# Wide and narrow matmuls of the queries, keys and MLP up halves in another order, and a last weight quarter stored 64 bytes later

## The chip, the cores and the metric

The kernel runs on one core of a Trainium2 chip. The metric is the device time of one execution in microseconds (us); lower is better. Before the change it is 740.41 us, the median of three runs between 740.17 and 740.46.

## The reference

An encoder trunk of two layers over 256 positions of 1024 features. Layer 0 mixes with two kinds of attention, layer 1 with a dilated attention of three head groups, and each is followed by an MLP:

```
for layer in range(2):
    xn = rms_norm(x, norm_mix[layer])
    x  = x + (even_mixer(xn, ...) if layer == 0 else odd_mixer(xn, ...))
    x  = x + square(relu(rms_norm(x, norm_mlp[layer]) @ w1[layer])) @ w2[layer]
return rms_norm(x, norm_final)

odd_mixer: hcat = xn @ w_in            # 3 groups x (queries, keys, values) x 16 heads x 64
           q, k = rope(q), rope(k)     # of every group
           out  = dilated_attention(q, k, v) @ w_o
```

The change touches two of these products: `xn @ w1` of both MLPs, and the queries and keys of `odd_mixer`.

## The kernel before, in words

**Split products.** Every matmul operand is a float32 value cut into a high part and a low remainder, and a product is taken as hi x hi + hi x lo + lo x hi. In the two places here that is done as a *wide* matmul, 512 moving columns, whose stationary operand is the high part of a weight tile and whose moving operand holds hi and lo of the activations side by side, and a *narrow* one, 256 columns, whose stationary operand is the low part of the weights. Both add up in one PSUM bank of 512 columns. With 1024 features in 8 tiles of 128 (`KT`), one tile of 128 output features needs 8 wide and 8 narrow matmuls.

**The weights' way.** A piece is 128 x 2048 floats. SyncE loads it (`load_weight`, L181), then ScalarE casts the high part into a tile `whi` (L215) and VectorE subtracts for the low part `wlo` (L216), each in four quarters of 512 columns (`split_piece`). Three `whi` and three `wlo` tiles exist; each is 128 columns larger than a piece, and `SHIFTS` says by how many floats a piece is moved inside its tile: `LINE`, 16 floats or 64 bytes, for the low part of `w1` and `w_oqk` (the queries' and keys' weights), nothing for their high part.

**The MLP's up half.** `up(j)`, 16 units in each MLP, makes 256 hidden features from one piece of `w1`: for j > 0 all 16 wide matmuls (L405), 8 for each of two banks, then all 16 narrow ones (L408). Unit 0 goes over the input features in three stretches, because these come late there.

**Queries and keys.** `qk_steps` makes one piece, two tiles of features (f = 0, 1), in four steps. For each f a step of 6 wide matmuls (L926), then one of 2 wide and 8 narrow (L929); f = 0 is then emptied from its PSUM bank by a copy on ScalarE (`side`, L934) and an addition on VectorE (L935), f = 1 by one reduction on VectorE (L937). Then `rope` turns the piece into queries or keys (L945 to L961). There are 8 units of heads with three pieces each, 24 pieces in all; `weave` puts the scores (L996), the transposes of the probabilities (L1016) and the mix with the values (L1027, L1032) of the unit before between the steps.

**What sets the order.** Each engine runs its instructions in one fixed order, made when the program is built, mostly that in which they are written; a `high_priority` block lets its instructions go ahead of others of their engine. Waits between engines are semaphores.

Of the kernel before, what the change touches and what calls it, by code (L numbers as in the profile page):

```python
# [17 lines left out]
F32R = mybir.dt.float32r  # L18
AF = mybir.ActivationFunctionType
ALU = mybir.AluOpType  # L20
# [3 lines left out]
P = 128  # L24
D = 1024
KT = D // P
T = 256
# [7 lines left out]
WCH = 2048  # L35
# [4 lines left out]
WPARTS = 4  # L40
NORM_PRIO = 300
# [2 lines left out]


LINE = 16
SHIFTS = {"w1": (0, LINE), "w_oqk": (0, LINE), "w_qk": (LINE, LINE), "w_oe": (LINE, LINE), "w_oo": (LINE, LINE)}

QK_ORDER = (0, 2, 1)
# [25 lines left out]
def trunk(ctx, tc, a, out):  # L75
    nc = tc.nc
# [8 lines left out]
    wsp = ctx.enter_context(tc.tile_pool(name="wsp", bufs=WBUFS))  # L85
    ps = ctx.enter_context(tc.tile_pool(name="ps", bufs=4, space=PSUM))

    def scratch(shape, name):

        n = int(np.prod(shape))  # L90
        v = work.tile([P, 512], F32, tag="scratch", name=name, bufs=12)[:, :n]
        if len(shape) == 2:
            v = v.rearrange("p (a b) -> p a b", b=shape[1])
        return v
# [13 lines left out]
    def bank(tag):  # L108
        return ps.tile([P, 512], F32, tag=tag, name=tag)
# [32 lines left out]
    specs = []  # L142

    def plan(name, n):
        for j in range(a[name].shape[0]):
            specs.append((a[name][j], n, SHIFTS.get(name, (0, 0))))

    def plan_mlp(layer):
        for j in (0, 1):
            specs.append((a["w1"][layer, j], WCH, SHIFTS["w1"]))  # L150
        for j in range(2, 16):
            specs.append((a["w1"][layer, j], WCH, SHIFTS["w1"]))
            specs.append((a["w2"][layer, j - 2], WCH, (0, 0)))
        for j in (14, 15):
            specs.append((a["w2"][layer, j], WCH, (0, 0)))

    CV = 416 + 512
    plan("w_cv", 2 * CV)
# [5 lines left out]
    plan("w_oe", 2 * D)  # L164
    plan_mlp(0)
    for kind, *at in odd_weights():
        specs.append((a[kind][tuple(at)], WCH, SHIFTS.get(kind, (0, 0))))
    plan("w_oo", 2 * D)
    plan_mlp(1)

    parts = {}
    state = {"loaded": 0, "split": 0, "used": 0}

    def load_weight(edges=None, earlier=lambda i: None):
        j = state["loaded"]
        src, n, _ = specs[j]
        raw = wraw.tile([P, WCH], F32, tag="raw", name="raw")
        edges = edges or (0, n)
        for i, c in enumerate(slice(*e) for e in zip(edges, edges[1:])):
            earlier(i)  # L180
            nc.sync.dma_start(raw[:, c], src[:, c])  # L181
        parts[j] = [raw, None, None]
        state["loaded"] = j + 1

    def split_tiles(j):
        return [wsp.tile([P, WCH + P], F32R, tag=n, name=n)[:, o:o + WCH] for n, o in zip(("whi", "wlo"), specs[j][2])]

    def cut(j, i, n):
        w = specs[j][1] // n
        return slice(i * w, (i + 1) * w)  # L190

    def split_piece(eng=None):
        j, i = divmod(state["split"], WPARTS)
        if i == 0:
            parts[j][1:] = split_tiles(j)
        raw, hi, lo = (z[:, cut(j, i, WPARTS)] for z in parts[j])
        state["split"] += 1
        return split(hi, lo, raw, eng)

# [49 lines left out]
    def two(z):  # L249
        return z.rearrange("p (f n) -> p f n", f=2)  # L250
# [137 lines left out]
    def mlp(mp, xT, s, invert, tail, make_down, beside=lambda j: None):  # L388


        hs = {}

        def up(j):
            w = weight()

            pu = [bank("w") for _ in range(2)]

            ranges = [range(4), range(4, 6), range(6, 8)] if j == 0 else [range(8)]  # L400
            cut_of = lambda k, f: slice(k * 256 + f * P, k * 256 + f * P + P)
            for ks in ranges:
                for f in range(2):
                    for k in ks:
                        nc.tensor.matmul(two(pu[f]), w[0][:, cut_of(k, f)], xT[2][:, k], start=k == 0, stop=False)  # L405
            for f in range(2):
                for k in range(KT):
                    nc.tensor.matmul(pu[f][:, 0:T], w[1][:, cut_of(k, f)], xT[0][:, k, :], start=False, stop=k == KT - 1)  # L408
            side, u = scratch([2, T], "side"), scratch([2, T], "u")
            for f in range(2):  # L410
                nc.scalar.copy(side[:, f], pu[f][:, T:2 * T])  # L411
                nc.vector.tensor_tensor(u[:, f], pu[f][:, 0:T], side[:, f], op=ALU.add)  # L412
            u, h = u.rearrange("p f n -> p (f n)"), scratch([512], "hsq")
            nc.vector.scalar_tensor_tensor(h, u, 0.0, u, ALU.max, ALU.mult)  # L414
            hs[j] = tuple(mp.tile([P, 512], F32R, tag=n, name=n, bufs=4) for n in ("hh", "hl"))
            split(*hs[j], h)

        squares = square_steps(s)
        for j in range(3):
            up(j)  # L420
            run_all(squares[2 * j - 2:2 * j])
        inv = invert()
        accs = open_accs()
        down = make_down(accs, hs)
        for j in range(tail[0]):
            w = weight()
            for f in range(2):
                down(j, w, f)
            if j + 3 < 16:
                up(j + 3)  # L430
            beside(j)
        return accs, hs, inv, {j: weight() for j in tail}
# [414 lines left out]
    def odd(op, xT, s):  # L847
        xh, xl, xp = xT
# [8 lines left out]
        for i in range(2):  # L857
            z = op.tile([P, 2, 4, P], F32, name=f"k12_{i}")
# [53 lines left out]
        def qk_steps(d, js=QK_ORDER):  # L912


            hold = {}

            def gemm(b, f, half):
                if f == 0 and half == 0:
                    hold["w"], hold["q"] = weight(), op.tile([P, 2, T], F32, tag="qk32", name="qk32", bufs=2)
                if half == 0:  # L920
                    hold["p"] = bank("acc")
                (wh, wl), pq, q32 = hold["w"], hold["p"], hold["q"]

                cut_of = lambda k: slice((f * KT + k) * P, (f * KT + k + 1) * P)
                for k in (range(0, 6), range(6, KT))[half]:
                    nc.tensor.matmul(two(pq), wh[:, cut_of(k)], xp[:, k], start=k == 0, stop=False)  # L926
                if half == 1:
                    for k in range(KT):
                        nc.tensor.matmul(pq[:, 0:T], wl[:, cut_of(k)], xh[:, k, :], start=False, stop=k == KT - 1)  # L929
                if half == 1:  # L930
                    with tc.high_priority(NORM_PRIO):
                        if f == 0:
                            side = scratch([T], "side")
                            nc.scalar.copy(side, pq[:, T:2 * T])  # L934
                            nc.vector.tensor_tensor(q32[:, f], pq[:, 0:T], side, op=ALU.add)  # L935
                        else:
                            nc.vector.tensor_reduce(q32[:, f], pq.rearrange("p (h n) -> p n h", h=2), axis=mybir.AxisListType.X, op=ALU.add)  # L937
                if f == 1 and half == 1:

                    with tc.high_priority(NORM_PRIO if b == QK_ORDER[-1] else 0):  # L940
                        rope(b, q32.rearrange("p f n -> p (f n)"))

            def rope(b, pq):

                sw, r1 = op.tile([P, 512], F32, tag="swap", name="sw", bufs=2), scratch([2, T], "r1")  # L945
                change = nc.scalar.copy if b == 1 else nc.sync.dma_start
                for r in range(0, P, 64):
                    change(sw[r:r + 32], pq[r + 32:r + 64])
                    change(sw[r + 32:r + 64], pq[r:r + 32])
                sw = sw.rearrange("p (f n) -> p f n", f=2)  # L950
                nc.vector.tensor_tensor(r1, pq.rearrange("p (f n) -> p f n", f=2), cosT.unsqueeze(1).broadcast_to([P, 2, T]), op=ALU.mult)
                nc.vector.tensor_tensor(sw, sw, sinT.unsqueeze(1).broadcast_to([P, 2, T]), op=ALU.mult)
                if b == 0:
                    nc.vector.tensor_tensor(r1, r1, sw, op=ALU.add)
                    split(d["q0h"], d["q0l"], r1)
                elif b == 1:
                    nc.vector.tensor_tensor(d["q12"], r1, sw, op=ALU.add)
                else:
                    for r in (0, 64):
                        cut = lambda z: z[r:r + 64].rearrange("p j (c n) -> p j c n", n=64)  # L960
                        nc.vector.tensor_tensor(d["k12"][r:r + 64, :, :, r:r + 64], cut(r1), cut(sw), op=ALU.add)  # L961

            return [lambda v=(b, f, h): gemm(*v) for b in js for f in range(2) for h in range(2)]

        def made_beside(plan, units):

# [97 lines left out]
        for u in range(7):  # L1064
            side = attend(u, units[u])
# [17 lines left out]
    xT, s = hand_over(accs, last, 1)  # L1083
# [103 lines left out]
```

## Time and profile before

| | |
|---|---|
| median of three runs | 740.41 us |
| the profiled execution | 740.37 us |
| its span, first to last instruction | 738.6 us |
| mean granted TensorE clock | 0.997 |
| PE (TensorE) busy | 730.7 us, 99% |
| PEld (TensorE weight loads) busy | 630.6 us, 85% |
| DVE (VectorE) busy | 540.8 us, 73% |
| ACT (ScalarE) busy | 471.3 us, 64% |

The 1.77 us between span and execution lie before the first and after the last instruction. Matmuls overlap on PE, so the length of one (390 ns for a wide one) is not its price; its price is the distance from its start to the start of the next. The chain of waits, which the profile follows back from the last instruction, gives it for runs of equal matmuls: a line `1.84 PE acc L926 x8` says that eight wide matmuls took 1.84 us from the start of the first to the start of what came next.

### The profile page before, as it was taken

The numbers are of one execution on the slowest core, as the hardware profiler recorded it, in microseconds if no ns is written. First come the engines' busy times: TensorE is split into PE (matmuls) and PEld (weight loads), VectorE is DVE, ScalarE is ACT, GpSimd is POOL, SyncE is SP. The second block draws the span as 40 slices with busy tenths as digits, with TensorE's granted clock in tenths as the row PEclk, the third lists the DMA queues.
The fourth block names the chain that finished last, engine by engine and source line by source line (L and its number), as shares of the span: only waits on it lengthen the run. The fifth ranks groups of instructions, "written<-read, shape, count | busy, mean of one in ns | idle before, by whom it ended". The sixth has DMA issues, their size and how long they took to land.

```text
span 738.6 us, 11982 instructions
## 1 busy us (share of the span) xinstructions
PE 730.7 (99%) x4539; PEld 630.6 (85%) x4539; DVE 540.8 (73%) x1100; ACT 471.3 (64%) x1020; POOL 8.3 (1%) x20
## 2 busy tenths in 40 slices
PE   9999999999999999999999999999999999999996
PEld 6998998888888887888888888888898888888885
DVE  6788859766665666789968886989559765665674
ACT  6788967554455456468877668687857455455441
POOL 0100000000000001000000000000000000000000
PEclk9999999999999999999999999999999999999998
DMA  8773335565555554645664544455546555555501
GB/s 288 319 256 116 115 114 172 178 222 171 193 206 177 199 195 154 232 156 178 205 226 147 207 160 179 143 192 175 181 159 221 180 174 197 193 177 189 210 1 57
DMA packets 24585, 133.17 MB, mean 180 GB/s; under 512 B 3664, under 2 KB 4816, under 8 KB 10192
## 3 DMA queue, kind: packets, MB, share of 16 engines
q1 hardware_dynamic: 24384, 132.28, 51.5%
q8 instruction: 35, 0.57, 0.3%
q14 instruction: 22, 0.18, 0.1%
q10 hardware_dynamic: 144, 0.13, 0.1%
HBM read 127.16 MB, written 1.05 MB: 174 GB/s over the span
## 4 chain that ended last, share of the span: by engine, by line
PE 96%; issue 1%; ACT 1%; DMA 1%; SPq 0%; DVE 0%; POOLq 0%; POOL 0%
PE w L405 16%; PE acc L219 13%; PE acc L220 13%; PE acc L221 13%; PE acc L926 12%; PE w L408 8%; PE acc L929 6%; PE acc L572 2%; PE w L228 1%; PE w L1016 1%; PE w L219 1%; PE w L783 1%; PE w L220 1%; PE w L221 1%; PE w L996 1%
## 5 line engine op out<-in xcount | busy, mean ns | idle before, releaser
L216 DVE TENSOR_TENSOR wlo<-raw,whi 128x512 fp32r<-128x512 f32 (+2 forms) x471 | 303.9, 682 | 68.8 <-ACT whi L215 68.0
L215 ACT CAST whi<-raw 128x512 fp32r<-128x512 f32 (+2 forms) x471 | 261.8, 614 | 138.2 <-PE acc L221 57.4
L405 PE MATMUL w<-pair,whi 128*128 128x512 f32 x512 | 122.0, 390 | 0.0
L405 PEld LDWEIGHTS w<-pair,whi 128*128 128x128 f32 x512 | 95.4, 188 | 20.1 <-DVE pair L256 0.6
L926 PE MATMUL acc<-pair,whi 128*128 128x512 f32 x384 | 100.9, 399 | 0.0
L219 PE MATMUL acc<-whi,hh 128*128 128x512 f32 x250 | 98.1, 392 | 0.0
L220 PE MATMUL acc<-wlo,hh 128*128 128x512 f32 x250 | 97.8, 391 | 0.0
L221 PE MATMUL acc<-whi,hl 128*128 128x512 f32 x250 | 97.6, 390 | 0.0
L926 PEld LDWEIGHTS acc<-pair,whi 128*128 128x128 f32 x384 | 67.7, 188 | 12.0 <-issue 0.2
L408 PEld LDWEIGHTS w<-pair,wlo 128*128 128x128 f32 x512 | 64.8, 189 | 2.5
L412 DVE TENSOR_TENSOR u<-w,side 128x256 f32<-128x256 f32 x64 | 27.0, 422 | 54.1 <-ACT side L411 53.8
L408 PE MATMUL w<-pair,wlo 128*128 128x256 f32 x512 | 65.5, 281 | 0.0
L215 ACT CAST hh<-hsq 128x512 fp32r<-128x512 f32 x32 | 19.9, 622 | 57.9 <-DVE hsq L414 57.9
L221 PEld LDWEIGHTS acc<-whi,hl 128*128 128x128 f32 x250 | 47.0, 188 | 9.8
L929 PEld LDWEIGHTS acc<-pair,wlo 128*128 128x128 f32 x384 | 51.8, 188 | 4.0
L219 PEld LDWEIGHTS acc<-whi,hh 128*128 128x128 f32 x250 | 47.1, 188 | 8.9
L220 PEld LDWEIGHTS acc<-wlo,hh 128*128 128x128 f32 x250 | 47.1, 188 | 8.6
L929 PE MATMUL acc<-pair,wlo 128*128 128x256 f32 x384 | 52.6, 280 | 0.0
L219 PE MATMUL acc<-whi,pair 128*128 128x512 f32 x80 | 32.3, 404 | 0.0
L220 PE MATMUL acc<-wlo,pair 128*128 128x512 f32 x80 | 31.3, 391 | 0.0
L221 PE MATMUL acc<-whi,pair 128*128 128x512 f32 x80 | 31.2, 390 | 0.0
L1005 DVE CUSTOM_DVE_ANT_0 sn<-w,mask 128x384 f32<-128x384 f32 x32 | 17.6, 551 | 10.9 <-PE w L996 10.9
(220 smaller groups left out, 1104.4 us busy)
## 6 DMA issues: line engine op xcount, KB each, us to landing
raw<-in_w SPq DMA_DIRECT2D x64, 1024.0 KB, 4.9
raw<-in_w_oqk SPq DMA_DIRECT2D x24, 1024.0 KB, 5.0
raw<-in_w_ov SPq DMA_DIRECT2D x12, 1024.0 KB, 5.0
raw<-in_w_qk SPq DMA_DIRECT2D x4, 1024.0 KB, 9.0
raw<-in_w_oe SPq DMA_DIRECT2D x4, 1024.0 KB, 5.0
sw<-qk SPq DMA_DIRECT2D x64, 64.0 KB, 2.0
raw<-in_w_oo SPq DMA_DIRECT2D x4, 1024.0 KB, 5.3
bias<-in_rpb SPq DMA_DIRECT2D x8, 256.0 KB, 3.7
```

The costliest lines, as they stand in the source:

```text
L215: a = nc.scalar.copy(hi, src).ins
L216: return a, (eng or nc.vector).tensor_tensor(lo, src, hi.bitcast(F32), op=ALU.subtract).ins
L219: nc.tensor.matmul(o, sh, mh, start=first, stop=False)
L220: nc.tensor.matmul(o, sh, ml, start=False, stop=False)
L221: nc.tensor.matmul(o, sl, mh, start=False, stop=last)
L405: nc.tensor.matmul(two(pu[f]), w[0][:, cut_of(k, f)], xT[2][:, k], start=k == 0, stop=False)
L408: nc.tensor.matmul(pu[f][:, 0:T], w[1][:, cut_of(k, f)], xT[0][:, k, :], start=False, stop=k == KT - 1)
L412: nc.vector.tensor_tensor(u[:, f], pu[f][:, 0:T], side[:, f], op=ALU.add)
L572: nc.tensor.matmul(o[:, 0:n], xs[i], (w[1], w[1], w[2])[i], start=(k, i) == (0, 0), stop=(k, i) == (KT - 1, 2))
L926: nc.tensor.matmul(two(pq), wh[:, cut_of(k)], xp[:, k], start=k == 0, stop=False)
L929: nc.tensor.matmul(pq[:, 0:T], wl[:, cut_of(k)], xh[:, k, :], start=False, stop=k == KT - 1)
L1005: nc.vector.tensor_tensor_reduce(out=sn, in0=ss[j][:, 0:384], in1=mask[:, i, :], op0=ALU.add, op1=ALU.min, scale=-(HD ** -0.5), scalar=3e3 ...
```

## The change

Three things, and no instruction is added or taken out.

1. **Order of a piece of queries and keys.** The four steps become: 6 wide of f = 0; 2 wide of f = 0 and 4 wide of f = 1; 4 wide of f = 1 and 4 narrow of f = 0; 4 narrow of f = 0, 8 narrow of f = 1, with the emptying of both banks and the rope. So 16 wide matmuls stand ahead of 16 narrow ones, on two PSUM banks, unless something is woven in.
2. **Order of the MLP's up half**, for j > 0: both f over the input features 0 to 5, then both over 6 and 7 (before: 0 to 7 of one f, then of the other). Still 16 wide, then 16 narrow.
3. **The last quarter of `whi`** of `w1` and `w_oqk` is stored 64 bytes later than the other three, and is read there. It is what the last four wide matmuls ahead of a narrow run load: input features 6 and 7 of both f in the MLP (unit 0 too), features 4 to 7 of f = 1 in the queries and keys.

```diff
@@ plan_mlp, and the same for the pieces of odd_weights() @@
-            specs.append((a["w1"][layer, j], WCH, SHIFTS["w1"]))
+            specs.append((a["w1"][layer, j], WCH, SHIFTS["w1"], True))
-        specs.append((a[kind][tuple(at)], WCH, SHIFTS.get(kind, (0, 0))))
+        specs.append((a[kind][tuple(at)], WCH, SHIFTS.get(kind, (0, 0)), kind == "w_oqk"))
@@ split_tiles, split_piece @@
+    def late(c):
+        return slice(c.start + LINE, c.stop + LINE)
...
+        if specs[j][3] and i == WPARTS - 1:
+            hi = parts[j][1][:, late(cut(j, i, WPARTS))]
@@ up @@
-            ranges = [range(4), range(4, 6), range(6, 8)] if j == 0 else [range(8)]
+            ranges = [range(4), range(4, 6), range(6, 8)] if j == 0 else [range(6), range(6, 8)]
...
-                        nc.tensor.matmul(two(pu[f]), w[0][:, cut_of(k, f)], xT[2][:, k], start=k == 0, stop=False)
+                        nc.tensor.matmul(two(pu[f]), w[0][:, late(cut_of(k, f)) if k >= 6 else cut_of(k, f)], xT[2][:, k], start=k == 0, stop=False)
@@ qk_steps @@
+            def wide(f, ks):
+                for k in ks:
+                    c = slice((f * KT + k) * P, (f * KT + k + 1) * P)
+                    nc.tensor.matmul(two(hold["p"][f]), hold["w"][0][:, late(c) if f == 1 and k >= 4 else c], xp[:, k], start=k == 0, stop=False)
...
+                if step == 0:
...
+                    hold["p"] = [bank("acc"), None]
+                    wide(0, range(0, 6))
+                elif step == 1:
+                    wide(0, range(6, KT))
+                    hold["p"][1] = bank("acc")
+                    wide(1, range(0, 4))
+                elif step == 2:
+                    wide(1, range(4, KT))
+                    narrow(0, range(0, 4))
+                else:
+                    narrow(0, range(4, KT))
+                    empty(0)
+                    narrow(1, range(KT))
+                    empty(1)
...
```

In the changed file the wide matmuls of the queries and keys are line L930, the narrow ones L935, the copy `side` L942; scores are L1022 instead of L996, transposes L1042 instead of L1016, the mix L1053 and L1058 instead of L1027 and L1032, the casts L225 instead of L215, the MLP's wide and narrow matmuls L415 and L418 instead of L405 and L408.

On TensorE, in the first unit of attention, right after the scores of unit 0 (`acc<-pair,whi` are wide matmuls, `acc<-pair,wlo` narrow ones, `w<-ident,pp` transposes). Before:

```order
L996 MATMUL w<-k_0_3258,q_3264 64x128 x8
L926 MATMUL acc<-pair,whi 128x512 x2
L929 MATMUL acc<-pair,wlo 128x256 x8
L926 MATMUL acc<-pair,whi 128x512 x8
L929 MATMUL acc<-pair,wlo 128x256 x8
L926 MATMUL acc<-pair,whi 128x512 x6
L1016 MATMUL w<-ident,pp 128x128 x3
L926 MATMUL acc<-pair,whi 128x512 x2
L929 MATMUL acc<-pair,wlo 128x256 x8
L1016 MATMUL w<-ident,pp 128x128 x3
L926 MATMUL acc<-pair,whi 128x512 x8
L929 MATMUL acc<-pair,wlo 128x256 x8
```
After:

```order
L1022 MATMUL w<-k_0_3258,q_3264 64x128 x8
L930 MATMUL acc<-pair,whi 128x512 x10
L935 MATMUL acc<-pair,wlo 128x256 x16
L930 MATMUL acc<-pair,whi 128x512 x6
L1042 MATMUL w<-ident,pp 128x128 x3
L930 MATMUL acc<-pair,whi 128x512 x6
L1042 MATMUL w<-ident,pp 128x128 x3
L930 MATMUL acc<-pair,whi 128x512 x4
L935 MATMUL acc<-pair,wlo 128x256 x16
```
The narrow matmuls stand in runs of 16 instead of 8, and the transposes between wide matmuls.

On TensorE again, one unit later, after scores and mix (`acc<-pts,v`). Before:

```order
L996 MATMUL w<-k_1_3260,q_3637 64x128 x8
L1027 MATMUL acc<-pts,v_3435 64x128 x4
L1032 MATMUL acc<-pts,v_3438 64x64 x4
L1027 MATMUL acc<-pts,v_3435 64x128 x4
L1032 MATMUL acc<-pts,v_3438 64x64 x4
L926 MATMUL acc<-pair,whi 128x512 x8
L929 MATMUL acc<-pair,wlo 128x256 x8
L926 MATMUL acc<-pair,whi 128x512 x8
L929 MATMUL acc<-pair,wlo 128x256 x8
L1016 MATMUL w<-ident,pp 128x128 x3
```
After:

```order
L1022 MATMUL w<-k_1_3260,q_3637 64x128 x8
L1053 MATMUL acc<-pts,v_3435 64x128 x4
L1058 MATMUL acc<-pts,v_3438 64x64 x4
L1053 MATMUL acc<-pts,v_3435 64x128 x4
L1058 MATMUL acc<-pts,v_3438 64x64 x4
L930 MATMUL acc<-pair,whi 128x512 x16
L935 MATMUL acc<-pair,wlo 128x256 x16
L1042 MATMUL w<-ident,pp 128x128 x3
L930 MATMUL acc<-pair,whi 128x512 x12
L1042 MATMUL w<-ident,pp 128x128 x3
```
Two runs of 8 wide and 8 narrow have become one of 16 and 16, and the transposes no longer follow a narrow run only.

On ScalarE in the middle of the queries and keys (`side<-acc` is the copy that empties f = 0, `whi<-raw` are casts of weight quarters, `pts<-w` copies of transposed probabilities). Before:

```order
L215 CAST whi<-raw 128x512 x4
L1018 COPY pts<-w 128x384
L934 COPY side<-acc 128x256
L1018 COPY pts<-w 128x384
L215 CAST whi<-raw 128x512 x4
L215 CAST q0h<-r_5149 128x512
L1018 COPY pts<-w 128x384
L934 COPY side<-acc 128x256
```
After:

```order
L225 CAST whi<-raw 128x512
L942 COPY side<-acc 128x256
L225 CAST whi<-raw 128x512 x3
L1044 COPY pts<-w 128x384 x2
L225 CAST whi<-raw 128x512 x2
L942 COPY side<-acc 128x256
L225 CAST whi<-raw 128x512 x2
```
The copy stands between casts of the next piece; it now comes near the end of its own.

## Rows read from the trace of the kernel before

**Rows 1.** The page: busy time by engine; the last chain's shares by engine, line.

```profile
PE 730.7 (99%) x4539; PEld 630.6 (85%) x4539; DVE 540.8 (73%) x1100; ACT 471.3 (64%) x1020; POOL 8.3 (1%) x20
...
PE 96%; issue 1%; ACT 1%; DMA 1%; SPq 0%; DVE 0%; POOLq 0%; POOL 0%
PE w L405 16%; PE acc L219 13%; PE acc L220 13%; PE acc L221 13%; PE acc L926 12%; PE w L408 8%; PE acc L929 6%; PE acc L572 2%; PE w L228 1%; PE w L1016 1%; PE w L219 1%; PE w L783 1%; PE w L220 1%; PE w L221 1%; PE w L996 1%
```

**Rows 2.** Costliest groups on the page: matmuls, count, busy us, mean ns.

```profile
L405 PE MATMUL w<-pair,whi 128*128 128x512 f32 x512 | 122.0, 390 | 0.0
...
L926 PE MATMUL acc<-pair,whi 128*128 128x512 f32 x384 | 100.9, 399 | 0.0
```

**Rows 3.** PE's load waits: line, releaser, total us, times, longest us.

```profile
PEld w L405 <- DVE pair L256: 0.6, 2, 0.4
...
PEld acc L926 <- issue: 0.2, 1, 0.2
```

**Rows 4.** The chain in time (start us, us, what): queries, keys, transposes.

```profile
320.79 1.84 PE acc L926 x8
322.62 0.94 PE acc L929 x8
...
348.58 1.86 PE acc L926 x8
```

**Rows 5.** The same chain after the scores and the mix of a unit.

```profile
360.63 0.23 PE acc L1032 x8
360.86 2.05 PE acc L926 x8
362.91 0.91 PE acc L929 x8
```

**Rows 6.** The chain in the second MLP: a settled unit of the up half.

```profile
588.20 3.62 PE w L405 x16
591.83 1.89 PE w L408 x16
```

**Rows 7.** The chain in the second MLP: its first units of up.

```profile
553.76 2.06 PE w L405 x9
...
555.82 2.15 PE w L405 x8
557.98 1.83 PE w L408 x16
```

**Rows 8.** PE's timeline (start us, us, what), last stage, operands not shifted.

```profile
728.12 0.28 PE L220 MATMUL w<-wlo,hh 128*128 128x256 f32 x1
...
732.20 0.28 PE L221 MATMUL w<-whi,hl 128*128 128x256 f32 x1
```

**Rows 9.** PE's timeline, first layer, narrow matmuls with shifted loads.

```profile
26.41 0.28 PE L220 MATMUL w<-pair,whi 128*128 128x256 f32 x1
...
30.41 0.28 PE L221 MATMUL w<-pair,wlo 128*128 128x256 f32 x1
...
31.10 0.28 PE L220 MATMUL w<-pair,whi 128*128 128x256 f32 x1
...
34.95 0.28 PE L221 MATMUL acc<-pair,wlo 128*128 128x256 f32 x1
...
35.32 0.36 PE L219 MATMUL acc<-pair,whi 128*128 128x256 f32 x1
35.52 0.28 PE L220 MATMUL acc<-pair,whi 128*128 128x256 f32 x1
```

**Rows 10.** The timeline of all engines where a unit's scores follow its last query.

```profile
475.83 0.68 DVE L957 TENSOR_TENSOR q<-r,sw 128x512 f32<-128x512 f32 x1
...
477.25 1.09 PE L996 MATMUL w<-k,q 128*64 128x128 f32 x16
```

**Rows 11.** Costliest groups on the page: the operations that split the weights.

```profile
L216 DVE TENSOR_TENSOR wlo<-raw,whi 128x512 fp32r<-128x512 f32 (+2 forms) x471 | 303.9, 682 | 68.8 <-ACT whi L215 68.0
L215 ACT CAST whi<-raw 128x512 fp32r<-128x512 f32 (+2 forms) x471 | 261.8, 614 | 138.2 <-PE acc L221 57.4
```

More of the change, by code (lines that the diff above doesn't have):

```diff
@@ L145, in plan @@
         for j in range(a[name].shape[0]):
-            specs.append((a[name][j], n, SHIFTS.get(name, (0, 0))))
+            specs.append((a[name][j], n, SHIFTS.get(name, (0, 0)), False))
     def plan_mlp(layer):
         for j in (0, 1):
-            specs.append((a["w1"][layer, j], WCH, SHIFTS["w1"]))
+            specs.append((a["w1"][layer, j], WCH, SHIFTS["w1"], True))
         for j in range(2, 16):
-            specs.append((a["w1"][layer, j], WCH, SHIFTS["w1"]))
-            specs.append((a["w2"][layer, j - 2], WCH, (0, 0)))
+            specs.append((a["w1"][layer, j], WCH, SHIFTS["w1"], True))
+            specs.append((a["w2"][layer, j - 2], WCH, (0, 0), False))
         for j in (14, 15):
-            specs.append((a["w2"][layer, j], WCH, (0, 0)))
+            specs.append((a["w2"][layer, j], WCH, (0, 0), False))
     CV = 416 + 512
@@ L175, in load_weight @@
         j = state["loaded"]
-        src, n, _ = specs[j]
+        src, n = specs[j][:2]
         raw = wraw.tile([P, WCH], F32, tag="raw", name="raw")
@@ L185, in split_tiles @@
     def split_tiles(j):
-        return [wsp.tile([P, WCH + P], F32R, tag=n, name=n)[:, o:o + WCH] for n, o in zip(("whi", "wlo"), specs[j][2])]
+        z = [wsp.tile([P, WCH + P], F32R, tag=n, name=n) for n in ("whi", "wlo")]
+        return [z[0][:, specs[j][2][0]:specs[j][2][0] + WCH + (LINE if specs[j][3] else 0)], z[1][:, specs[j][2][1]:specs[j][2][1] + WCH]]
+    def late(c):
+        return slice(c.start + LINE, c.stop + LINE)
     def cut(j, i, n):
@@ L915, in qk_steps @@
             hold = {}
-            def gemm(b, f, half):
-                if f == 0 and half == 0:
-                    hold["w"], hold["q"] = weight(), op.tile([P, 2, T], F32, tag="qk32", name="qk32", bufs=2)
[L920 to L938, printed above, removed]
@@ new lines, in wide, with narrow @@
+            def wide(f, ks):
+                for k in ks:
+                    c = slice((f * KT + k) * P, (f * KT + k + 1) * P)
+                    nc.tensor.matmul(two(hold["p"][f]), hold["w"][0][:, late(c) if f == 1 and k >= 4 else c], xp[:, k], start=k == 0, stop=False)
+            def narrow(f, ks):
+                for k in ks:
+                    c = slice((f * KT + k) * P, (f * KT + k + 1) * P)
+                    nc.tensor.matmul(hold["p"][f][:, 0:T], hold["w"][1][:, c], xh[:, k, :], start=False, stop=k == KT - 1)
@@ new lines, in empty @@
+            def empty(f):
+                pq, q32 = hold["p"][f], hold["q"]
+                with tc.high_priority(NORM_PRIO):
+                    if f == 0:
+                        side = scratch([T], "side")
+                        nc.scalar.copy(side, pq[:, T:2 * T])
+                        nc.vector.tensor_tensor(q32[:, f], pq[:, 0:T], side, op=ALU.add)
+                    else:
+                        nc.vector.tensor_reduce(q32[:, f], pq.rearrange("p (h n) -> p n h", h=2), axis=mybir.AxisListType.X, op=ALU.add)
@@ new lines, in gemm @@
+            def gemm(b, step):
+                if step == 0:
+                    hold["w"], hold["q"] = weight(), op.tile([P, 2, T], F32, tag="qk32", name="qk32", bufs=2)
+                    hold["p"] = [bank("acc"), None]
[7 more added lines that the diff above has]
+                    narrow(0, range(0, 4))
+                else:
+                    narrow(0, range(4, KT))
+                    empty(0)
+                    narrow(1, range(KT))
+                    empty(1)
@@ L940, in gemm @@
                     with tc.high_priority(NORM_PRIO if b == QK_ORDER[-1] else 0):
-                        rope(b, q32.rearrange("p f n -> p (f n)"))
+                        rope(b, hold["q"].rearrange("p f n -> p (f n)"))
             def rope(b, pq):
@@ L961, in rope @@
                         nc.vector.tensor_tensor(d["k12"][r:r + 64, :, :, r:r + 64], cut(r1), cut(sw), op=ALU.add)
-            return [lambda v=(b, f, h): gemm(*v) for b in js for f in range(2) for h in range(2)]
+            return [lambda v=(b, i): gemm(*v) for b in js for i in range(4)]
         def made_beside(plan, units):
```

## The prediction

> **What bounds the kernel now.** I read the page first. PE is busy for 99% of the span, and the chain that ended last runs on PE for 96% of it [rows 1]. In the page's costliest groups the wide matmuls of the two places that the change touches stand among the first, 512 of L405 and 384 of L926, with no idle time ahead of them [rows 2]; as many narrow ones, L408 and L929, belong to them. Their shares of the chain are 16 + 8 + 12 + 6 = 42% [rows 1], 310 us. Then I asked for the waits of the weight loads: the largest that touches these lines is 0.6 us in two waits, for activations, and for the queries and keys 0.2 us of "issue" [rows 3]. So no other engine holds PE up there, and the change can only be worth what it does to the pace of PE itself. For that I read the chain in order of time, which gives how long a run of equal matmuls took from its first start to the next start.
>
> **Paces that the trace shows.** A settled wide matmul: 16 in 3.62 us, 0.2263 each [rows 6]. Eight wide after eight narrow take 1.84 us where 8 x 0.2263 is 1.81, so starting again after narrow ones costs 0.03; after transposes 1.86, 0.05 [rows 4]; after a unit's scores and mix 2.05, 0.24 [rows 5]. A narrow matmul has more than one pace, and it holds for a whole run. After settled wide ones 16 take 1.89 us [rows 6] and 8 take 0.94 [rows 4]; after wide ones that were disturbed just before, 8 take 0.91 [rows 5], and in the second MLP 16 take 1.83 behind 17 wide that needed 2.06 + 2.15 us instead of 3.85 [rows 7]. The timeline of the first layer, where the loads are moved by the same 64 bytes, shows both paces ahead of and behind a short break: 34 starts from 26.41 to 30.41 us, 0.1176 each, and 34 from 31.10 to 34.95, 0.1132 each. In the last stage, where no operand is moved, it is 34 starts from 728.12 to 732.20, 0.1200 each [rows 8, 9]. So the same shape of matmul runs at 0.1200, 0.1176 or 0.1132 us without any wait, and what differs is where its loads lie and what ran just ahead. I read that as a phase between loads and matmuls, which a disturbance of a few ns can move.
>
> **The change part by part.** The sum is made against the profiled run, 740.37 us (738.6 of span and 1.77 around it), next to the median of 740.41.
>
> *Turns between wide and narrow.* By the order of instructions the queries and keys turn from narrow back to wide 32 times before and 14 times after. 18 x 0.03 = **-0.5 us**. From transposes to wide they turn 19 times before and 14 after, 5 x 0.05 = -0.25, but five transposes now end in front of narrow ones: a first narrow one behind transposes took 0.20 from start to start (35.32 to 35.52) instead of 0.115 [rows 9], 5 x 0.085 = +0.4. The two leave between -0.25 and +0.4, and I take 0.1. The turn behind scores and mix stays, six times.
>
> *The pace of the narrow runs.* The four wide matmuls ahead of every narrow run now load weights that lie 64 bytes later than those of the wide ones before them. The trace has no such switch inside a wide run. Its nearest rows are disturbed wide runs, behind which narrow ones go at 0.1132 [rows 5, 7, 9], and undisturbed ones, behind which they go at 0.1176 [rows 4, 6]. I take the fast pace, since four matmuls with another address right ahead of the run are a disturbance at the place where one decides. MLP: 32 runs of 16 x (0.1176 - 0.1132) = 0.07 each; the one at 557.98 us is fast already: 31 x 0.07 = **-2.2 us**. Queries and keys: of 48 runs of 8 the chain shows 31 at about 0.94 and 17 at about 0.91, together 44.6 us; 384 x 0.1132 = 43.5: **-1.1 us**. If the pace stays, both are 0; if it falls back to that of rows 8, see the third rival.
>
> *The late wide matmuls themselves*, 4 x 32 in the MLPs and 4 x 24 in the queries and keys, 224. If their own turn costs what starting after transposes costs (0.05 for 8, 0.006 each), +1.4. If moving loads helps wide ones as it helps narrow ones (0.1200 against 0.1176, 0.0024 each), -0.5. Neither row is the case itself; I take **+0.6 us**, nearer to the cost, because the gain above needs them to be disturbed. The reordering of f and k in the MLP's up half keeps 16 wide ahead of 16 narrow and the same two banks; the address of a load jumps there between every two matmuls, before as after, and by itself I cost it at nothing.
>
> *Two banks at a time, and the emptying.* No split grows or is added: they stay 471 operations on each engine, of 614 and 682 ns [rows 11], and run about two pieces ahead of PE. The copy and the addition that empty f = 0 come later in the piece; on ScalarE some casts of later pieces now go ahead of that copy, and who waits is the rope and then the scores. They are covered by the eight narrow ones of f = 1 (0.94 us) [rows 4] and by the slack ahead of the scores: in the tightest unit the last query is written at 475.83 + 0.68 = 476.51 us and the scores start at 477.25, 0.74 us later [rows 10]. I cost it at nothing. If a cast of 0.614 [rows 11] stands in front and the cover is gone, up to 0.7 us at each of the two units whose slack is under a microsecond, +1.4.
>
> *Sum.* -0.5 + 0.1 - 2.2 - 1.1 + 0.6 = -3.1; 740.4 - 3.1 = **737.3 us**. With both ends of the unknown terms: -0.5 - 0.25 - 3.3 - 0.5 = -4.55 (735.8) to -0.5 + 0.4 - 3.3 + 1.4 = -2.0 (738.4), and 1.4 more with a late rope.
>
> **The rivals.**
>
> *Nothing moves in the pace.* The trace shows settled runs at one pace in place after place [rows 4, 6], and a run of two wide ones more may let it settle again whatever the address. For it speaks that the low parts are moved already and the narrow runs that follow are still at 0.1176. Then the turns give -0.5, the 17 fast runs of 8 in the queries and keys partly lose their 0.03 (up to +0.5, since longer wide runs settle more often), and the late ones cost nothing: -0.3, **740.1 us**. Against it speak rows 8 and 9. The Trainium skill, page "SBUF — State Buffer", section "Who interferes with whom", gives PE two read ports, one for moving data and one for weight loads, independent of each other, and lets only VectorE and GpSimd contend; by that, where the weights lie changes nothing, and the time is this rival's. The trace does not bear it out fully: it has one shape at three paces with no wait named, though that alone does not prove that the address is the cause.
>
> *Only one of the two places.* The MLP has settled runs throughout, the queries and keys are broken up by transposes and scores. With the MLP alone at the fast pace: -0.5 - 2.2 + 0.3 = -2.4, 738.0; with the queries and keys alone: -0.5 - 1.1 + 0.3 = -1.3, **739.1**.
>
> *Slower: the phase goes the wrong way.* The late loads put the narrow runs at the pace of rows 8, 0.1200. MLP: 32 x 16 x 0.0024 = +1.2; queries and keys: 384 x 0.1200 = 46.1 against 44.6, +1.5; with the late wide ones +0.6 and the turns -0.4: +2.9, **743.3 us**. The turn and the late ones nearly cancel, and each nanosecond on the 896 narrow ones is 0.9 us, so it decides from about 1.5 ns on. Against it: no run with moved low parts in these rows goes at 0.1200.
>
> **How the numbers follow.** This kernel's measurement can tell about 0.2%, 1.5 us, from no change: same is 738.9 to 741.9. Forecast 0.46, no change in pace 0.31, one place only 0.10 (0.06 of it under 738.9), slower 0.13. Faster 0.46 + 0.06 = 0.52, same 0.31 + 0.04 = 0.35, slower 0.13. The range from 735.8 to 740.6 holds the forecast, the second case and most of the first rival, some 0.83; the likeliest case alone is 735.8 to 738.4.
>
> **What would show it.** Right: in the chain, L418 x16 at 1.81 to 1.83 us in nearly all 32 units instead of 1.89, L935 x16 at about 1.83, and L415 x16 at 3.62 to 3.66. Wrong: L418 x16 at 1.89 (first rival), or 1.92 (third). A rope that comes too late would stand in the waits of the loads at L1022, behind VectorE. The prediction falls if the late wide matmuls cost more than 0.02 us each, which none of the rows shows outside scores and mix, or if the pace of the narrow runs is set by something other than what runs right ahead.

## The result, and the profile after

The changed kernel takes 741.85 us (median of 22 runs), the kernel before 740.42 in as many: a ratio of 1.0019, 95% interval 1.0013 to 1.0025. It is 1.4 us slower; 737.3 was forecast. It stands at the upper edge of what the prediction called "same", outside the predicted range.

The profiled execution took 741.32 us with a span of 739.5. The page still says that PE is the bound. Busy times by engine, and shares of the last chain by engine, answering [rows 1]:

```profile
PE 731.6 (99%) x4539; PEld 631.5 (85%) x4539; DVE 541.8 (73%) x1103; ACT 468.4 (63%) x1017; POOL 8.3 (1%) x20
...
PE 96%; issue 1%; ACT 1%; DMA 1%; SPq 0%; DVE 0%; POOLq 0%; POOL 0%
```

Most of the loss is in PE's pace, and the chain in order of time (start us, us, what) shows it. In the second MLP, a settled unit, answering [rows 6]:

```profile
588.82 3.65 PE w L415 x16
592.47 1.89 PE w L418 x16
...
599.83 3.65 PE w L415 x16
603.48 1.89 PE w L418 x16
```

The 16 wide matmuls take 3.65 us instead of 3.62, and the narrow ones did not move from 1.89. A cut inside the first of these runs, the chain of the changed kernel from 591.31 us on:

```profile
591.31 1.16 PE w L415 x5
592.47 0.23 PE w L418 x2
```

The first eleven took 591.31 - 588.82 = 2.49 us, 0.2264 each, as before. The last five, one on time and the four late ones, took 1.16 where five settled ones take 1.13. From start to start the late ones are 0.236, 0.231, 0.236 and 0.231 us.

The disturbed first unit of that MLP, answering [rows 7], had its narrow run fast before, and still has:

```profile
554.29 4.21 PE w L415 x17
558.50 1.82 PE w L418 x16
```

In the queries and keys, answering [rows 4], runs behind narrow ones and one behind transposes:

```profile
318.39 0.94 PE acc L930 x4
319.33 1.83 PE acc L935 x16
...
326.72 3.68 PE acc L930 x16
330.40 1.89 PE acc L935 x16
```

Sixteen wide behind narrow ones take 3.68, that is 3.62 + 0.03 for the turn + 0.03 for the four late ones, and the narrow run is slow; the run at 319.33, behind only four wide ones that had not come into step, is fast.

Adding up, for every matmul of a line, the time from its start to the next start on PE gives the account by lines. The last two columns are experiments told below:

| us of PE | before | changed | nothing late | one late |
|---|---|---|---|---|
| wide, MLP up (512) | 116.80 | 117.62 | 116.78 | 117.49 |
| narrow, MLP up (512) | 60.31 | 60.24 | 60.32 | 58.26 |
| wide, queries and keys (384) | 91.31 | 90.92 | 90.48 | 90.63 |
| narrow, queries and keys (384) | 45.07 | 45.45 | 45.43 | 44.64 |
| scores of two heads (`two_heads`), with the wait ahead of the rest of the scores (144) | 11.62 | 11.78 | 12.59 | 11.97 |

From first to last start PE needs 731.95 us instead of 731.01. Of these 0.94, the MLP's wide ones are +0.82, its narrow ones -0.07; the queries and keys come out even, -0.39 and +0.38; the scores are +0.16. The rest of the difference of the medians, 0.5, is not in this one execution and is not shown by it; the experiment with a short rope tests one candidate.

### The profile page after: what moved, and what is told of

It reads as the page before. It is cut to its first block, busy times and chain, and to the rows that moved or that the text cites. A ratio compares the mean times of both kernels' runs of the same rounds, so it can differ in the third digit from the quotient of the medians.

```text
span 739.5 us, 11966 instructions
## 1 busy us (share of the span) xinstructions
PE 731.6 (99%) x4539; PEld 631.5 (85%) x4539; DVE 541.8 (73%) x1103; ACT 468.4 (63%) x1017; POOL 8.3 (1%) x20
## 4 chain that ended last, share of the span: by engine, by line
PE 96%; issue 1%; ACT 1%; DMA 1%; SPq 0%; DVE 0%; POOLq 0%; POOL 0%
PE w L415 16%; PE acc L229 13%; PE acc L230 13%; PE acc L231 13%; PE acc L930 12%; PE w L418 8%; PE acc L935 6%; PE acc L582 2%; PE w L238 1%; PE w L1042 1%; PE w L229 1%; PE w L793 1%; PE w L230 1%; PE w L231 1%; PE w L1022 1%
## 5 line engine op out<-in xcount | busy, mean ns | idle before, releaser
L225 ACT CAST whi<-raw 128x512 fp32r<-128x512 f32 (+2 forms) x471 | 263.7, 614 | 143.1 <-issue 57.2
L415 PE MATMUL w<-pair,whi 128*128 128x512 f32 x512 | 122.8, 392 | 0.0
L415 PEld LDWEIGHTS w<-pair,whi 128*128 128x128 f32 x512 | 95.4, 188 | 20.4 <-DVE pair L266 0.6
L930 PE MATMUL acc<-pair,whi 128*128 128x512 f32 x384 | 96.8, 399 | 0.0
L930 PEld LDWEIGHTS acc<-pair,whi 128*128 128x128 f32 x384 | 69.5, 188 | 13.8 <-issue 0.2
L418 PEld LDWEIGHTS w<-pair,wlo 128*128 128x128 f32 x512 | 64.7, 189 | 2.9
L418 PE MATMUL w<-pair,wlo 128*128 128x256 f32 x512 | 65.5, 281 | 0.0
L225 ACT CAST hh<-hsq 128x512 fp32r<-128x512 f32 x32 | 19.9, 621 | 57.9 <-DVE hsq L424 57.9
L935 PEld LDWEIGHTS acc<-pair,wlo 128*128 128x128 f32 x384 | 48.5, 189 | 2.2
L935 PE MATMUL acc<-pair,wlo 128*128 128x256 f32 x384 | 49.9, 281 | 0.0
L1033 ACT ACTIVATE pp<-sn,dmn 128x384 f32<-128x384 f32 x32 | 19.6, 613 | 10.1 <-DVE dmn L1031 9.3
```

Of the source, the lines that this page charges most:

```text
L225: a = nc.scalar.copy(hi, src).ins
L415: nc.tensor.matmul(two(pu[f]), w[0][:, late(cut_of(k, f)) if k >= 6 else cut_of(k, f)], xT[2][:, k], start=k == 0, stop=False)
L930: nc.tensor.matmul(two(hold["p"][f]), hold["w"][0][:, late(c) if f == 1 and k >= 4 else c], xp[:, k], start=k == 0, stop=False)
L935: nc.tensor.matmul(hold["p"][f][:, 0:T], hold["w"][1][:, c], xh[:, k, :], start=False, stop=k == KT - 1)
L1033: nc.scalar.activation(pp, sn, AF.Exp, bias=mn, scale=-1.0, accum_out=z)
```

## Experiments

The theories on the loss: the new address of the last quarter costs the time (A), or the new order does (B). And on why the narrow runs did not get faster: four late matmuls are long enough to come into step again where one is not (C, later L), or the step of the last wide matmul decides (D).

**The order alone.** All that is late is taken back; every engine runs the same instructions in the same order as in the changed kernel.

```diff
-            hi = parts[j][1][:, late(cut(j, i, WPARTS))]      # last quarter of w1, w_oqk
+            (stored with the other three)
-... w[0][:, late(cut_of(k, f)) if k >= 6 else cut_of(k, f)]
+... w[0][:, cut_of(k, f)]
-... hold["w"][0][:, late(c) if f == 1 and k >= 4 else c]
+... hold["w"][0][:, c]
```

> The changed kernel's order of instructions, engine by engine, with no weight quarter moved. In the trace of the changed kernel the four late wide matmuls take 0.236, 0.231, 0.236, 0.231 us instead of 0.2266, 0.027 us a unit (L415 x16 is 3.65 instead of 3.62). Theory A, the address costs this: L415 x16 is 3.62 again in the settled units, L930 x16 3.65 behind narrow ones instead of 3.68, the narrow runs stay at 1.89; 56 groups x 0.027 = 1.5 us less than the changed kernel, about 740.3, the same as before within 0.2 us or up to 0.5 us faster by the fewer turns. Theory B, the new order costs it (alternating banks, jumps in the features): the 16 wide stay at 3.65 and the time at 741.3 to 741.9.

It took 740.45 us, 1.0001 of before (0.9992 to 1.0009). Its chain, the same unit of the MLP and one piece of queries and keys:

```profile
326.15 3.65 PE acc L930 x16
329.80 1.89 PE acc L935 x16
...
588.59 3.63 PE w L415 x16
592.21 1.89 PE w L418 x16
```

Theory A holds: with the address the extra 0.03 of a group is gone, and so are 1.4 us; the order by itself neither costs nor gains more than the 0.6 us that the interval leaves. That it gains nothing, though its wide matmuls save 0.83 us (91.31 to 90.48), has two reasons in the table. The narrow ones lose 0.36 (45.07 to 45.43): five of them now come first behind transposes and take 0.20 us from start to start instead of 0.116, 0.42 in all, while inside the runs the mean step stays at 0.116. And the scores waited. The waits of its loads, where the kernel before has no such row and the changed one only the second:

```profile
PEld w L1022 <- DVE q L983: 0.9, 1, 0.9
...
PEld w L1022 <- issue: 0.3, 1, 0.3
```

**Late in the MLPs alone.**

```diff
-        specs.append((a[kind][tuple(at)], WCH, SHIFTS.get(kind, (0, 0)), kind == "w_oqk"))
+        specs.append((a[kind][tuple(at)], WCH, SHIFTS.get(kind, (0, 0)), False))
```

> The changed kernel with the late quarter in the MLPs alone; the queries and keys keep the new order without it. Theory A (address): L415 x16 stays 3.65, L930 x16 behind narrow ones goes from 3.68 to 3.65; 24 x 0.027 = 0.65 less than the changed kernel, about 741.2. Theory B (order): no difference to the changed kernel, 741.3 to 741.9.

741.13 us, 1.0009 (1.0000 to 1.0018). The time alone hardly parts the theories, since 741.2 was expected by A and at least 741.3 by B; the chain does:

```profile
326.79 3.65 PE acc L930 x16
...
589.05 3.65 PE w L415 x16
```

The MLPs keep their late 3.65, and the queries and keys are back from 3.68 to 3.65. The three medians form a ladder: nothing late 740.45, MLPs late +0.68 (32 x 0.027 = 0.86 expected), queries and keys late as well +0.72 (0.65 expected). That agrees with theory A, within intervals of some 0.6 us on each median.

**The whole high part of w1 moved.** Order as above, nothing late.

```diff
-SHIFTS = {"w1": (0, LINE), ...
+SHIFTS = {"w1": (LINE, LINE), ...
```

> The order of the changed kernel, nothing late, but the whole high part of w1 moved by 64 bytes, as its low part is. If it is the address itself that is slow against the activations, all 16 wide matmuls of a unit run at 0.2335: L415 x16 3.74, 32 x 0.11 = 3.5 us more than with nothing late, 743.8. If it is only the switch of address within a run, which lasts about four matmuls, L415 x16 settles at 3.62 to 3.65 and the time is 740 to 741.

742.92 us, 1.0033 (1.0021 to 1.0044). Its chain in the second MLP:

```profile
589.62 3.73 PE w L415 x16
593.35 1.89 PE w L418 x16
```

All 16 run at 0.236 and 0.231 in turn, without end: it is not the switch that costs but the address, 3.73 - 3.63 = 0.10 us a unit, by the sums of starts 3.1 us in all (116.78 to 119.88). The medians differ by 2.5, less than the 3.5 expected; in the profiles part of that is the 0.8 us by which the scores waited with the order alone and which is missing here. Loads that lie 64 bytes further against the same activations make a wide matmul 0.007 us slower, with no wait in the trace. The Trainium skill, page "SBUF — State Buffer", section "Who interferes with whom", which the prediction weighed, has PE's two read ports independent of each other; the prediction took from it that where the weights lie changes nothing. The trace disagrees with that reading: the other engines run the same instructions in both kernels, and the 64 bytes are worth 0.10 us a unit. Whether the ports are independent it does not show.

**One late matmul instead of four.** The quarters of these pieces become 640, 640, 640 and 128 columns, so that only the last wide matmul ahead of a narrow run is late.

```diff
-        w = specs[j][1] // n
+        w = 640 if specs[j][3] else specs[j][1] // n
-... late(cut_of(k, f)) if k >= 6 else cut_of(k, f)
+... late(cut_of(k, f)) if (k, f) == (7, 1) else cut_of(k, f)
-... late(c) if f == 1 and k >= 4 else c
+... late(c) if f == 1 and k >= 7 else c
```

> The changed kernel with only the last wide matmul of a run late (128 columns of the piece; the quarters of these pieces are 640, 640, 640 and 128 wide, no operation more). Theory A: one slow matmul, at most 0.01 us a group, 56 x 0.01 = +0.5 over nothing late, about 740.8, narrow runs at 1.89. Theory C, which is what is left of the prediction: narrow runs go at the fast pace when the wide ones ahead end out of step, and four late ones are long enough to come into step again (0.236, 0.231, 0.236, 0.231 repeats), one is not: L418 x16 is 1.82, 56 x 0.07 = -3.9 + 0.5, about 737.3.

738.49 us, 0.9973 (0.9962 to 0.9983): faster than both kernels. Its chain in the second MLP:

```profile
587.03 3.63 PE w L415 x16
590.67 1.82 PE w L418 x16
...
597.95 3.63 PE w L415 x16
601.59 1.82 PE w L418 x16
```

This is what the prediction had described: narrow runs at 1.82. The MLPs' gained 60.31 - 58.26 = 2.05 us and paid 0.7 with their wide ones. In the queries and keys some runs stayed slow, as the one behind the scores of the first unit, in the same chain:

```profile
340.27 2.53 PE acc L930 x10
342.79 1.89 PE acc L935 x16
```

The late matmul there, the last of the ten, took 0.225 us from start to start: the address alone does not make the step long, and behind the short step the narrow run is slow.

**Two late, three late.** Both walk, in the MLPs, over the features 0 to 6 of both tiles and then 7, so that the late ones are the last; the four parts in which a piece is cast and subtracted are cut to fit, as with one late (not in the diff).

```diff
-... [range(6), range(6, 8)]
+... [range(7), range(7, 8)]
-... late(cut_of(k, f)) if k >= 6 else cut_of(k, f)
+... late(cut_of(k, f)) if k >= 7 else cut_of(k, f)            # two
+... late(cut_of(k, f)) if 2 * k + f >= 13 else cut_of(k, f)   # three
-... late(c) if f == 1 and k >= 4 else c
+... late(c) if f == 1 and k >= 6 else c                        # two
+... late(c) if f == 1 and k >= 5 else c                        # three
```

> As the changed kernel, but only the last two wide matmuls ahead of a narrow run are late. Seen so far: late wide matmuls run in a rhythm of 0.236, 0.231, 0.236, 0.231 us; the narrow run behind four of them is slow (L418 x16 1.89), behind one of them fast (1.82). Theory D, the step decides: a narrow run is fast when the last wide one took 0.236 and slow when it took 0.231, so an even number late is slow: L418 x16 1.89, two late cost 0.013 a group, 741.0. Theory L, the length decides: one or two late are a disturbance, four are long enough to settle: L418 x16 1.82, about 738.7.

> The same with the last three wide matmuls late. Theory D (the step decides): they end on 0.236, so L418 x16 is 1.82 and L415 x16 3.65: three late cost 0.023 a group, 56 x 0.023 = 1.3, against 0.5 for one: about 739.3. Theory L (the length decides): three are nearer to four than to one, L418 x16 1.89, about 741.5.

Two late: 741.16 us, 1.0005 (0.9996 to 1.0014). Three late: 738.49 us, 0.9970 (0.9959 to 0.9982). The chain of two late, then that of three late:

```profile
589.38 3.64 PE w L415 x16
593.02 1.89 PE w L418 x16
```

```profile
587.39 3.65 PE w L415 x16
591.04 1.82 PE w L418 x16
```

This is theory D: not how many are late decides, but on which step the last one ends. Late ones go 0.236, 0.231, 0.236, 0.231; one and three end on 0.236 and the narrow run is fast, two and four end on 0.231 and it is slow. Three late pay as much for their wide matmuls as four do (3.65) and still win 2 us. The rule goes beyond the late ones. In the profiles of the kernel before, the changed one and the six experiments so far, 472 narrow runs start straight behind a wide matmul. Taking the mean step in the second half of each run, over 0.116 us for slow: of 302 behind a step of at most 0.231 us, 300 are slow; of 170 behind one of at least 0.232, 166 are fast. In the four profiles that follow it holds less well on the long side: 56 of 57 are slow, and 130 of 143 fast. Eight of those 13 misses are in the run with 128 bytes, and six are behind a step of exactly 0.232, so the line between the two is not sharp.

**Is it the odd 64 bytes?** One late, but by 128 bytes.

```diff
-        return slice(c.start + LINE, c.stop + LINE)
+        return slice(c.start + 2 * LINE, c.stop + 2 * LINE)
```

> The kernel with one late wide matmul, but that part of the weights 128 bytes later instead of 64. If any other address is a disturbance, the last wide one takes 0.236 again and L418 x16 is 1.82, 738.5. If it is the odd 64 bytes that make a wide load slow against its activations, 128 bytes are as good as none: the last wide one takes 0.226, L418 x16 is 1.89, 740.5.

739.26 us, 0.9981 (0.9972 to 0.9990). Its chain in the second MLP:

```profile
587.75 3.64 PE w L415 x16
591.39 1.82 PE w L418 x16
```

So 128 bytes disturb too; from start to start the last two wide ones now take 0.232 or 0.233, and then 0.234. The second guess, that only an odd 64 bytes does it, falls. It gains 0.8 us less than 64 bytes, half of that in the narrow ones of the queries and keys (45.03 instead of 44.64), where 10 of 24 runs stay slow.

**The MLPs without the new order.** The kernel before, with one late matmul a unit in the MLPs and its queries and keys untouched.

```diff
 # kernel before
-... w[0][:, cut_of(k, f)]
+... w[0][:, late(cut_of(k, f)) if (k, f) == (7, 1) else cut_of(k, f)]
```

> The kernel before, queries and keys in the order of before and nothing late there; only the last wide matmul of each unit of the MLPs' up half is late, with the order of features of before. If the gain of the kernel with one late comes from the MLPs alone: 32 x (0.069 - 0.009) = 1.9 us, 738.6. If it needs the new order of the queries and keys too, it stays over 739.5. The scores do not wait for the rope here as they may in the new order (0.2 to 0.9 us in the runs so far).

739.47 us, 0.9984 (0.9975 to 0.9993), though its narrow runs are as fast as with one late everywhere:

```profile
587.86 3.63 PE w L415 x16
591.49 1.82 PE w L418 x16
```

The gain is 1.1 us where 1.9 was expected: by the sums of starts its narrow ones gain 2.04 (60.31 to 58.27), nearly as expected, but its wide ones pay 0.72 (116.80 to 117.52) instead of 0.3, more than half of it in the first two units of each MLP (the settled ones pay 0.009 each, as expected), and the scores 0.14. So the MLPs make about half of the 2 us and the queries and keys, order and one late together, the other half.

**A short rope.** The order alone, with the queries of groups 1 and 2 made without the swapped half.

```diff
             def rope(b, pq):
+                if b == 1:
+                    return nc.vector.tensor_tensor(d["q12"], ..., cosT..., op=ALU.mult)
```

> The kernel with the new order and nothing late, and without the swap half of the rope in the queries of groups 1 and 2 (piece b = 1: q = q * cos alone; four copies on ScalarE and two operations on VectorE left out in each of the 8 units), so that these queries are ready some 3 us earlier and the scores can't wait for them. In that kernel's profile the scores of one unit waited 0.8 us longer for these queries than before. If such waits are what eats the saved turns of the new order (91.31 to 90.48 us of wide matmuls), the wait is gone and the time is 0.5 to 0.9 us below the 740.45 of the order alone: 739.5 to 739.9. If they are an accident of one execution, it stays at 740.3 to 740.5.

739.88 us, 0.9992 (0.9983 to 1.0001), against 740.45 with the whole rope: 0.6 us less, as expected if such waits eat the saved turns. In its profile the row of the scores in the table is 11.62 again, as before. Where it sits is the place of [rows 10]. The timeline of the order alone (start us, us, engine, line, what) at the scores of that unit:

```profile
476.39 0.68 DVE L226 TENSOR_TENSOR wlo<-raw,whi 128x512 fp32r<-128x512 f32 x1
...
476.99 0.68 DVE L983 TENSOR_TENSOR q<-r,sw 128x512 f32<-128x512 f32 x1
...
477.73 1.09 PE L1022 MATMUL w<-k,q 128*64 128x128 f32 x16 [0.72 <-DVE q L983]
```

The query is written at 476.99 + 0.68 = 477.67 us, 1.16 later than before, behind a split of weights, and PE waits for it. In the profiled run of the changed kernel the same query was written at 477.25 and the scores started at 477.86, so the wait did not arise there. Of the eight profiles with the steps of the change and the whole rope it stands in two, this one and that with the MLPs late. The short rope also takes operations from ScalarE and VectorE, so the 0.6 is the wait and whatever else these held up.

**Another cut of the steps.** One late, but 12 wide as the first step, 4 wide and all narrow ones as the second, two empty steps.

```diff
-                    wide(0, range(0, 6))                        # step 0
+                    wide(0, range(KT)); wide(1, range(0, 4))    # step 0
-                    ... three more steps
+                    wide(1, range(4, KT)); narrow(0, range(KT)); empty(0); narrow(1, range(KT)); empty(1)   # step 1, with the rope
```

> The kernel with one late wide matmul (738.5), with the steps of a piece of queries and keys cut anew: 12 wide, then 4 wide and all 16 narrow with the emptying and the rope, then two empty steps, so that transposes fall between the 12th and 13th wide one or between two pieces, no longer into a narrow run or ahead of 10 wide ones. In the profile of the one-late kernel some 11 of the 24 pieces had a narrow run at 0.118 or broken by transposes. If all those run at 0.1135: about 8 x 0.07 + 5 x 0.09 = 1.0 us less, 737.5. If the later transposes hold up the mix or the scores instead, no gain or a loss: 738.5 or more.

740.78 us, 1.0008 (0.9999 to 1.0016), 2.3 us slower than one late with the steps of the change. Its narrow runs are the fastest of all (44.37 us in the queries and keys), but the scores of one unit waited 1.4 us, by the waits of its loads:

```profile
PEld w L1017 <- issue: 1.4, 1, 1.4
```

and its chain ahead of them runs through the rope of the keys and its swap by DMA:

```profile
352.13 3.14 DMA sw<-qk
...
358.52 0.70 DVE k L982
359.22 0.14 issue
359.35 0.62 PE w L1017 x6
```

The other end of its forecast came true. By the sums of starts the narrow ones of the queries and keys gave 0.27 us more (44.64 to 44.37), and the scores, the transposes and the mix, with the waits ahead of them, took 2.3.

## Why the prediction was wrong, step by step

**What bounds the kernel** was right: 1.4 us were lost with PE busy 99%. Of the 0.94 that one profile shows, 0.74 is pace and turns, and 0.16 the scores.

**The turns** were right. Counting what a wide run takes over 0.2265 us for each matmul, the runs behind narrow ones cost 1.00 us before and 0.52 with the order alone: 0.48 less, 0.5 was taken. The runs behind transposes saved 0.40, and the five narrow ones that now come first behind transposes cost 0.42: together nothing, 0.1 was taken.

**The pace of the narrow runs is the step that failed.** The prediction took the fast pace "since four matmuls with another address right ahead of the run are a disturbance at the place where one decides". The rows bore out that disturbed wide runs are followed by fast narrow ones, and one late matmul does make them so in the MLPs. But four end where none would have ended, on the slow side. Of the 3.3 us that the term was worth, 0.07 came in the MLPs and nothing in the queries and keys; the 0.38 that these lost are the five turns behind transposes (0.42), and their mean step inside a run is 0.116 in both kernels. The chain has the sign that the prediction itself named for this, L418 x16 at 1.89. The rows to read were there: [rows 4] and [rows 5] show only that eight wide ones behind scores are followed by 0.91, not on which step they end; start by start in the trace of before, the last step tells slow from fast in 78 of 80 runs.

**The late wide matmuls** were mis-sized: +0.6 was taken from between -0.5 and +1.4. Against the order alone they cost 0.84 us in the MLPs and 0.44 in the queries and keys, 1.3, or 0.0057 each. The upper bound, 0.006 each, was close by luck: it was the price of starting again behind transposes, and the run with all of w1's high part moved shows that what is paid for is the address, for as long as it lasts, and not a start.

**The rope** was put at nothing, with up to 0.7 us at a unit as its bound if the cover was gone. It is gone in some executions: 0.8 us of extra wait at the named unit in the profile of the order alone, 0.5 in that with the MLPs late, none there in that of the changed kernel (0.16 at another unit), and 0.6 by the medians of the short rope. How much of the changed kernel's median it makes stays open.

**The rivals.** "Nothing moves in the pace" came nearest: it had the pace of the narrow runs right, and took the late ones as free, which is 1.3 us of its miss of 1.75. "Only one of the two places" fell, since neither moved. The slower rival expected the pace of [rows 8], 0.1200, which no narrow run of 16 shows here; the time came out slower by another way.

With the measured terms the sum is: turns -0.83 + 0.42 = -0.4, pace of the narrow runs -0.1, late ones +1.3, rope +0.2 (the changed kernel's profile) to +1.0 (that of the order alone, scores in all), between +0.9 and +1.7; measured +1.4.

## What to carry to other kernels

When two paces of the same instruction stand in a trace, find out start by start what precedes each before counting on one of them; an average over eight hides it. A disturbance that is meant to put a pipeline out of step has to be tried in several lengths, because its rhythm may repeat: here one and three gained 2 us, two gained nothing (1.0005) and four lost 1.4. And a new order on a saturated engine is also a new deadline for everyone who feeds it: in two profiles the saved turns were paid back in waits for a rope that had 0.7 us of slack before.

## What the runs showed of the hardware

The granted clock was 0.997 to 0.999 in all twelve profiles. A settled wide matmul, 512 columns, takes 0.2264 us from start to start, or 0.236 and 0.231 in turn, by where in SBUF its weights lie, 64 bytes apart, with the same activations and no wait in the profile. The address is not alone in this: in the kernel before, unmoved wide ones behind narrow ones take 0.231, 0.236, 0.228, 0.233 and 0.231 us from 320.62 us on, and then 0.226.

A narrow one, 256 columns, runs at 0.118 or 0.1135 in most runs from the first matmul to the last, and which of the two follows the step of the wide one ahead: at most 0.231 us, slow, at least 0.232, fast, in 466 of 472 runs, and in 186 of 200 in the four profiles behind these. Theory D, which rests on it, had two and three late ones right before they ran. What in the engine makes it so the runs do not show, and none of them moved the weights of the narrow ones.
